# A two-layer encoder step on one core: part of the retention scores in float32r halves, 32 stationary columns for the sample, shared temporaries

## The chip, the cores and the metric

The kernel runs on one core of one Trainium2 chip. The metric is the device time in microseconds (us) of one execution. The time before is the median of three runs, 2776.84 us (2776.18 to 2777.35).

## What is computed

The reference is one inference step of a two-layer encoder on 256 prompt frames and 32 sample frames, 2048 wide. Layer 0 mixes frames by a gated MLP, layer 1 by retention; each is followed by a SwiGLU block, and every sublayer by a layer norm. The change lies in the retention of layer 1, which per head does, for one block of frames:

```python
q = rope(heads(q, RET_DK), pos) * (RET_DK ** -0.5)
k = rope(heads(k, RET_DK), pos)
...
scores = jnp.einsum('bhqd,bhkd->bhqk', q, k) * decay[None]
intra = jnp.einsum('bhqk,bhkv->bhqv', scores, v)
cross = jnp.einsum('bhqd,bhdv->bhqv', q, s0) * inner[None, :, :, None]
s_new = blk_decay[None, :, None, None] * s0 + jnp.einsum(
    'bhkd,bhkv->bhdv', k * zeta[None, :, :, None], v)
```

There are 8 heads with 256 channels of q and k and 512 of v. The kernel takes the prompt's 256 frames in one piece and the sample's 32 frames beside them, so 288 columns go through everything.

## The kernel before

**Matmuls in halves.** All large matmuls run on float32r operands, a float32 format that TensorE (PE) streams in one pass. To keep accuracy, an operand is split into a high half (`hi`, a cast on ScalarE, ACT) and a low half (`lo = x - hi`, a subtraction on VectorE, DVE); `split` at L449 to L451 does both. A product is then three matmuls: hi by hi, hi by lo, lo by hi (L106 to L108). The weights arrive in chunks of eight 128x128 blocks; `prep` loads a chunk three chunks ahead and splits it into `whi` and `wlo`. `turned` and `mm4` (L171 to L179) only give the moving columns another order of reading.

**Order of work.** PE's order is that of the code. A "tick" passes after each output tile of 128 rows (16 steps of three matmuls, L106 to L108); `core.after(n, f)` calls `f` n ticks later, so that the short matmuls of a head stand between the tiles of the large projection `ab_in`. The order on DVE and ACT is made by a scheduler when the kernel is built; the rows of the trace stand in that order.

**A head of the retention** (class `Head`). `evac` gets the finished tiles. When both tiles of k, and then of q, are done, `turn` rotates them (`rope`, L661 to L669, on DVE) into `r` (`rk`, `rq`); with k it starts `k_move`, which sends k through DRAM to have it by rows (`kw`). With q it makes the scaled sample's q (`qf`, and its halves `qi`), and asks for `scores` after two ticks (three for head 0). `k_split` (L741 to L759) makes the scaled halves `kh`, `kl`, `ks` from `kw`, also after two ticks. `scores` (L761) issues three groups of float32 matmuls into one PSUM bank: keys 0 to 127 with all 256 queries (L766), keys 128 to 255 with the second 128 queries (L768), and the sample's 32 frames (L770), for which `rk` held the sample's k three times side by side, so that 96 stationary columns give the scores on three groups of 32 partitions. The results are multiplied by the decay table (`pf`, `psf`) and split into `ph`, `pl` and `pss` (shown as `r_ps`), from which `attend`, one tick later, computes the outputs.

**Temporaries.** `prev` is the layer norm ahead of the retention; `prev.tmp` gives a buffer of 288 columns out of six that are used in turn. In the kernel before, the retention had buffers of its own for `zero`, `rt1`, `rt2`, `qf`, `pf` and `psf`.

Of the kernel before, what the change touches and what calls it, by code (L numbers as in the profile page):

```python
# [10 lines left out]
F32 = mybir.dt.float32  # L11
# [616 lines left out]
def retention(core, cst, x, y, lnp, prev, ins, st_p_out, st_s_out):  # L628
# [4 lines left out]
    with ExitStack() as es:  # L633
# [14 lines left out]
        zero = pool.tile([P, NS], F32, name="r_zero")  # L648
# [12 lines left out]
        def rope(dst, a, b, cos, sin, nm):  # L661
            t1 = pool.tile([P, NT], F32, tag="rt1", name=f"rt1{nm}", bufs=1)
            t2 = pool.tile([P, NT], F32, tag="rt2", name=f"rt2{nm}", bufs=1)
            nc.vector.tensor_tensor(t1, a[:, :NT], cos, ALU.mult)
            nc.vector.tensor_tensor(t2, b[:, :NT], sin, ALU.mult)
            nc.vector.tensor_tensor(dst[:, 0, :NT], t1, t2, ALU.subtract)
            nc.vector.tensor_tensor(t1, a[:, :NT], sin, ALU.mult)
            nc.vector.tensor_tensor(t2, b[:, :NT], cos, ALU.mult)
            nc.vector.tensor_tensor(dst[:, 1, :NT], t1, t2, ALU.add)  # L669

        class Head:
# [33 lines left out]
            def turn(self, m, ps):  # L705
                h = self.h
                isk = m >= 16
                nm = ("k" if isk else "q") + str(h)
                r = pool.tile([P, 2, NP + (NR if isk else NS)], F32, tag="kr" if isk else "qr", name="r" + nm)
                rope(r, ps[0], ps[1], cs[:, 0, :], cs[:, 1, :], nm)  # L710
                if isk:
                    self.kr = r
                    nc.scalar.copy(r[:, :, NT:].rearrange("p d (r n) -> p d r n", r=2),
                                   r[:, :, NP:NT].unsqueeze(2).broadcast_to([P, 2, 2, NS]))
                    self.k_move()
                else:
                    self.qr = r
                    qf = pool.tile([P, 2, NS], F32, tag="qf", name=f"qf{h}")
                    qi = pool.tile([P, 160], F32R, tag="qi", name=f"qi{h}")
                    self.qi = qi[:, 20:20 + 4 * NS].rearrange("p (d a n) -> p d a n", d=2, a=2)  # L720
                    nc.vector.tensor_tensor(qf, r[:, :, NP:], inn[:, h, :].unsqueeze(1).broadcast_to([P, 2, NS]), ALU.mult)
                    split(nc, self.qi[:, :, 0, :], self.qi[:, :, 1, :], qf)
                    core.after(self.wait, self.scores)
# [37 lines left out]
            def scores(self):  # L761
# [3 lines left out]
                for d in range(2):  # L765
                    mm(b[:, 0:NP], self.kr[:, d, 0:P], self.qr[:, d, 0:NP], start=d == 0, stop=d == 1)  # L766
                for d in range(2):
                    mm(b[:, NP:NP + P], self.kr[:, d, P:NP], self.qr[:, d, P:NP], start=d == 0, stop=d == 1)  # L768
                for d in range(2):
                    mm(b[:NR, 384:384 + NS], self.kr[:, d, NP:], self.qr[:, d, NP:], start=d == 0, stop=d == 1)  # L770
                pf = pool.tile([P, 384], F32, tag="pf", name=f"pf{h}")
                self.ph = pool.tile([P, 384], F32R, tag="ph", name=f"ph{h}")
                self.pl = pool.tile([P, 384], F32R, tag="pl", name=f"pl{h}")
                psf = pool.tile([P, NS], F32, tag="psf", name=f"psf{h}")
                nc.vector.tensor_tensor(pf[:, :NP], b[:, :NP], self.dec[:, :NP], ALU.mult)
                nc.vector.tensor_tensor(pf[:, NP:], b[:, NP:384], self.dec[:, :P], ALU.mult)
                nc.vector.tensor_tensor(psf[:NR, :], b[:NR, 384:384 + NS], self.dec[:NR, NP:], ALU.mult)
                r = slice(2 * NS, NR)
                nc.scalar.copy(pss[:NR, :NS], psf[:NR, :])
                nc.vector.tensor_tensor(pss[r, :NS], psf[r, :], pss[r, :NS].bitcast(F32), ALU.subtract)  # L780
                split(nc, self.ph, self.pl, pf)
# [278 lines left out]
```

## Time and profile before

| | |
|---|---|
| median of three runs | 2776.84 us |
| the profiled execution, its own time | 2779.29 us |
| its span, first to last instruction | 2777.5 us |
| granted TensorE clock, mean | 0.999 |
| PE, busy share of the span | 100% |
| DVE, busy share | 60% |
| ACT, busy share | 45% |
| scores, first to last start on PE | 1212.3 to 1810.3 us |

A row of the order of time has the start, the duration, the engine (PE for matmuls, PEld for their weight loads), the line, the operation, and what is written from what; `x4` are four equal instructions merged, and a bracket holds the idle time ahead and what ended it. A group's row has its busy time and the mean duration in ns behind the first bar. A row of stretches has the length and then, for PE, PEld, DVE, ACT and POOL, the busy time and the count, the granted clock, the DMA share and GB/s. Matmuls overlap, so the distance between starts says what a matmul costs PE, and the duration does not.

### The profile page before, as it was taken

Reading aid. Unit: us, or ns where it says so; the run is one execution under the profiler, and the core shown is the slowest. Engines: PE = TensorE matmul, PEld = TensorE weight load, DVE = VectorE, ACT = ScalarE, POOL = GpSimd, SP = SyncE. Lnnn points to the kernel's source line nnn. Section 1 sums busy time; section 2 is a strip of 40 time slices with the busy share of each in tenths; the row PEclk is TensorE's granted clock in tenths of the full one; section 3 lists DMA queues with packets and bytes.
Section 4 is the critical chain, followed back from the end, with each engine's and each line's share of the span. In section 5 each row is a group of like instructions: output and inputs, shape, how many; then the busy total and the mean of one; then the engine's idle time right before and its main releaser. Section 6 shows DMA issues by size and latency. Waiting matters only on the chain.

```text
span 2777.5 us, 51381 instructions
## 1 busy us (share of the span) xinstructions
PE 2764.5 (100%) x21574; PEld 2750.9 (99%) x21574; DVE 1665.4 (60%) x2358; ACT 1241.7 (45%) x1645; POOL 141.3 (5%) x241
## 2 busy tenths in 40 slices
PE   9999999999999999999999999999999999999998
PEld 9999999999999999999999999999999999999998
DVE  5688854445444466767765666767844445444465
ACT  5465643433334344644543444445633433333343
POOL 1100000000000000012200111200000000000001
PEclk9999999999999999999999999999999999999999
DMA  7655455555555555567765666755555555555553
GB/s 270 217 189 166 166 178 175 172 172 174 175 175 175 172 175 178 189 205 236 230 198 173 200 216 214 232 194 175 168 174 174 175 174 173 172 173 175 175 174 126
DMA packets 147672, 515.49 MB, mean 186 GB/s; under 512 B 18080, under 2 KB 22448, under 8 KB 147408
## 3 DMA queue, kind: packets, MB, share of 16 engines
q1 hardware_dynamic: 133072, 473.47, 51.1%
q0 software_dynamic: 14224, 38.59, 4.7%
q8 instruction: 168, 2.75, 0.4%
q14 instruction: 64, 0.52, 0.0%
q10 hardware_dynamic: 144, 0.15, 0.0%
HBM read 486.98 MB, written 25.17 MB: 184 GB/s over the span
## 4 chain that ended last, share of the span: by engine, by line
PE 98%; DVE 1%; DMA 1%; issue 0%; ACT 0%; POOL 0%; SPq 0%; DVEq 0%; POOLq 0%
PE af_in L107 13%; PE af_in L108 13%; PE af_in L106 13%; PE ab_in L106 7%; PE ab_in L107 7%; PE ab_in L108 7%; PE af_out L106 6%; PE af_out L107 6%; PE af_out L108 6%; PE ab_out L107 2%; PE ab_out L106 2%; PE ab_out L108 2%; PE aa_in L108 2%; PE aa_in L106 2%; PE aa_in L107 2%; PE aa_out L106 1%
## 5 line engine op out<-in xcount | busy, mean ns | idle before, releaser
L451 DVE TENSOR_TENSOR wlo<-raw,whi 128x1024 fp32r<-128x1024 f32 (+1 forms) x892 | 1086.0, 1218 | 883.6 <-ACT whi L450 879.4
L450 ACT CAST whi<-raw 128x1024 fp32r<-128x1024 f32 (+1 forms) x892 | 933.1, 1047 | 1382.8 <-issue 336.5
L107 PE MATMUL af_in<-xl,whi 128*128 128x288 f32 (+1 forms) x2816 | 812.6, 289 | 0.0
L106 PE MATMUL af_in<-xh,whi 128*128 128x288 f32 (+1 forms) x2816 | 812.3, 288 | 0.0
L108 PE MATMUL af_in<-xh,wlo 128*128 128x288 f32 (+1 forms) x2816 | 812.3, 288 | 0.0
L108 PEld LDWEIGHTS af_in<-xh,wlo 128*128 128x128 f32 x2816 | 527.7, 187 | 0.0
L107 PEld LDWEIGHTS af_in<-xl,whi 128*128 128x128 f32 x2816 | 527.7, 187 | 0.0
L106 PEld LDWEIGHTS af_in<-xh,whi 128*128 128x128 f32 x2816 | 527.7, 187 | 0.0
L106 PE MATMUL ab_in<-xh,whi 128*128 128x288 f32 (+1 forms) x1536 | 443.9, 289 | 0.0
L107 PE MATMUL ab_in<-xl,whi 128*128 128x288 f32 (+1 forms) x1536 | 443.3, 289 | 0.0
L108 PE MATMUL ab_in<-xh,wlo 128*128 128x288 f32 (+1 forms) x1536 | 443.2, 289 | 0.0
L108 PE MATMUL af_out<-hh,wlo 128*128 128x288 f32 x1408 | 405.9, 288 | 0.0
L106 PE MATMUL af_out<-hh,whi 128*128 128x288 f32 x1408 | 405.9, 288 | 0.0
L107 PE MATMUL af_out<-hl,whi 128*128 128x288 f32 x1408 | 405.9, 288 | 0.0
L107 PEld LDWEIGHTS ab_in<-xl,whi 128*128 128x128 f32 x1536 | 287.9, 187 | 0.3
L106 PEld LDWEIGHTS ab_in<-xh,whi 128*128 128x128 f32 x1536 | 287.9, 187 | 0.3
L108 PEld LDWEIGHTS ab_in<-xh,wlo 128*128 128x128 f32 x1536 | 287.9, 187 | 0.0
L107 PEld LDWEIGHTS af_out<-hl,whi 128*128 128x128 f32 x1408 | 263.8, 187 | 0.0
L108 PEld LDWEIGHTS af_out<-hh,wlo 128*128 128x128 f32 x1408 | 263.8, 187 | 0.0
L106 PEld LDWEIGHTS af_out<-hh,whi 128*128 128x128 f32 x1408 | 263.8, 187 | 0.0
L108 PE MATMUL aa_in<-xh,wlo 128*128 128x288 f32 x512 | 148.4, 290 | 1.2 <-DVE wlo L451 1.2
L106 PE MATMUL aa_in<-xh,whi 128*128 128x288 f32 x512 | 148.7, 290 | 0.1
(240 smaller groups left out, 2867.0 us busy)
## 6 DMA issues: line engine op xcount, KB each, us to landing
raw<-in_wpack_dram SPq DMA_DIRECT2D x887, 512.0 KB, 3.3
v_room<-tv POOLq DMA_DIRECT2D x32, 144.0 KB, 5.0
of<-o_room POOLq DMA_DIRECT2D x32, 144.0 KB, 5.3
vw<-v_room POOLq DMA_DIRECT2D x8, 512.0 KB, 5.3
out_st_s_dram<-sso POOLq DMA_DIRECT2D x16, 256.0 KB, 2.6
out_st_p_dram<-so POOLq DMA_DIRECT2D x16, 256.0 KB, 2.9
o_room<-to POOLq DMA_DIRECT2D x8, 512.0 KB, 3.8
y<-in_xT_dram SPq DMA_DIRECT2D x8, 288.0 KB, 5.5
```

The costliest lines, as they stand in the source:

```text
L106: mm(ps, hi, xh, start=first, stop=False)
L107: mm(ps, hi, xl, start=False, stop=False)
L108: mm(ps, lo, xh, start=False, stop=last)
L450: nc.scalar.copy(hi, f)
L451: nc.vector.tensor_tensor(lo, f, hi.bitcast(F32), ALU.subtract)
```

## The change

Three things change. The scores of the first 128 keys, two float32 matmuls (four passes in the trace, since each float32 matmul shows as two) become six float32r matmuls: k's columns 0 to 127 and q's columns 0 to 255 are split into halves (`k1a`, `k1b`, `q1a`, `q1b` for head 1; `a` is the high half). The sample's scores take 32 stationary columns and not 96, so k's threefold copy goes, and the three partition groups of `pss` are filled from one result of 32 partitions. The small temporaries come from `prev.tmp`; `pf` becomes two tiles, split one after the other.

PE's order at head 1, before and then after (`sc` is the bank of the scores):

```order
L108 MATMUL ab_in_192_14178<-xh,wlo_14106 128x3x24x4
L766 MATMUL sc_14244<-rq_14164,rk_14002 128x256 x2
L768 MATMUL sc_14244<-rq_14164,rk_14002 128x128 x2
L770 MATMUL sc_14244<-rq_14164,rk_14002 96x32 x2
L106 MATMUL ab_in_193_14262<-xh,whi_14135 128x3x24x4
```

```order
L108 MATMUL ab_in_192_14200<-xh,wlo_14124 128x3x24x4
L179 MATMUL sc_14266<-q1a,k1a 128x4x16x4
L179 MATMUL sc_14266<-q1b,k1a 128x4x16x4
L179 MATMUL sc_14266<-q1a,k1b 128x4x16x4
L179 MATMUL sc_14266<-q1a,k1a 128x4x16x4
L179 MATMUL sc_14266<-q1b,k1a 128x4x16x4
L179 MATMUL sc_14266<-q1a,k1b 128x4x16x4
L773 MATMUL sc_14266<-rq_14182,rk_14017 128x128 x2
L775 MATMUL sc_14266<-rq_14182,rk_14017 32x32 x2
L106 MATMUL ab_in_193_14292<-xh,whi_14153 128x3x24x4
```

The place among the tiles of the projection is the same; the first operands are now halves, and `q1b` is read by the second matmul.

DVE's order at head 1, from the last step of q's rotation to the first product with the decay, before and then after (`tv` is a transposition of the next projection tile, `wlo` a weight chunk's low half):

```order
L669 TENSOR_TENSOR rq_14164<-rt1q_14165,rt2q_14166 128x288
L721 TENSOR_TENSOR qf_14173<-rq_14164,r_inn 128x64
L451 TENSOR_TENSOR wlo_14211<-raw_14209,whi_14210 128x1024
L752 SCALAR_TENSOR_TENSOR kl_14091<-kw_14015,r_zt,kh_14090 128x128 x4
L758 SCALAR_TENSOR_TENSOR ks_14092<-kw_14015,r_zt,ks_14092 32x128 x2
L451 TENSOR_TENSOR qi_14174<-qf_14173,qi_14174 128x2x32
L696 STREAM_TRANSPOSE tv_14242<-ab_in_192_14178 128x9x32
L451 TENSOR_TENSOR wlo_14265<-raw_14263,whi_14264 128x1024
L775 TENSOR_TENSOR pf_14251<-sc_14244,dec_13280 128x256
```

```order
L669 TENSOR_TENSOR rq_14182<-rt1q_1_14185,rt2q_1_14186 128x288
L722 TENSOR_TENSOR qf_1_14193<-rq_14182,r_inn 128x64
L451 TENSOR_TENSOR wlo_14233<-raw_14231,whi_14232 128x1024
L755 SCALAR_TENSOR_TENSOR kl_14109<-kw_14031,r_zt,kh_14108 128x128 x4
L761 SCALAR_TENSOR_TENSOR ks_14110<-kw_14031,r_zt,ks_14110 32x128 x2
L451 TENSOR_TENSOR qi_14194<-qf_1_14193,qi_14194 128x2x32
L451 TENSOR_TENSOR q1b<-rq_14182,q1a 128x512
L696 STREAM_TRANSPOSE tv_14264<-ab_in_192_14200 128x9x32
L451 TENSOR_TENSOR wlo_14295<-raw_14293,whi_14294 128x1024
L780 TENSOR_TENSOR pf_1_14277<-sc_14266,dec_13283 128x256
```

One row is new, `q1b`, behind `kl`, `ks` and `qi`. In all of heads 1 to 7 `q1b`'s counterpart stands right behind `qi`, which is right behind `ks`.

ACT's order at head 1 and, behind the dots, at head 2, both after the change:

```order
L450 CAST whi_14232<-raw_14231 128x1024
L450 CAST qi_14194<-qf_1_14193 128x2x32
L450 CAST q1a<-rq_14182 128x512
L753 ACTIVATE kh_14108<-kw_14031,r_zt 128x256 x2
L759 ACTIVATE ks_14110<-kw_14031,r_zt 32x256 x2
L450 CAST whi_14294<-raw_14293 128x1024
...
L450 CAST whi_14931<-raw_14930 128x1024
L753 ACTIVATE kh_14807<-kw_14730,r_zt 128x256 x2
L759 ACTIVATE ks_14809<-kw_14730,r_zt 32x256 x2
L450 CAST qi_14893<-qf_1_14892 128x2x32
L450 CAST q2a<-rq_14881 128x512
L450 CAST whi_14993<-raw_14992 128x1024
```

`q1a` and `q2a` are the new rows; the others stand in the same order as before, so that in heads 1, 4, 5 and 6 `kh` and `ks` come behind the new cast, and in heads 2, 3 and 7 ahead of it.

```diff
@@ -645,7 +645,7 @@
         nc.gpsimd.dma_start(inn, ins["inner"])
         ln = PostNorm(core, cst, x, y, lnp, 2)
         pss = pool.tile([P, 2 * NS], F32R, tag="pss", name="r_ps")
-        zero = pool.tile([P, NS], F32, name="r_zero")
+        zero = prev.tmp("r_zero")[:, :NS]
         nc.gpsimd.memset(zero, 0.0)
         nc.scalar.copy(pss[:NR, NS:], zero[:NR, :])
         heads = {}
@@ -659,8 +659,8 @@
             return t[:, :4 * NT].rearrange("p (b i s) -> p b i s", b=9, i=4)
 
         def rope(dst, a, b, cos, sin, nm):
-            t1 = pool.tile([P, NT], F32, tag="rt1", name=f"rt1{nm}", bufs=1)
-            t2 = pool.tile([P, NT], F32, tag="rt2", name=f"rt2{nm}", bufs=1)
+            t1 = prev.tmp(f"rt1{nm}")
+            t2 = prev.tmp(f"rt2{nm}")
             nc.vector.tensor_tensor(t1, a[:, :NT], cos, ALU.mult)
             nc.vector.tensor_tensor(t2, b[:, :NT], sin, ALU.mult)
             nc.vector.tensor_tensor(dst[:, 0, :NT], t1, t2, ALU.subtract)
@@ -706,20 +706,23 @@
                 h = self.h
                 isk = m >= 16
                 nm = ("k" if isk else "q") + str(h)
-                r = pool.tile([P, 2, NP + (NR if isk else NS)], F32, tag="kr" if isk else "qr", name="r" + nm)
+                r = pool.tile([P, 2, NT], F32, tag="kr" if isk else "qr", name="r" + nm)
+                parts = [pool.tile([P, 2, P if isk else NP], F32R, tag=nm[0] + x, name=nm + x) for x in "ab"]
                 rope(r, ps[0], ps[1], cs[:, 0, :], cs[:, 1, :], nm)
                 if isk:
                     self.kr = r
-                    nc.scalar.copy(r[:, :, NT:].rearrange("p d (r n) -> p d r n", r=2),
-                                   r[:, :, NP:NT].unsqueeze(2).broadcast_to([P, 2, 2, NS]))
                     self.k_move()
+                    self.kp = parts
+                    split(nc, *parts, r[:, :, :P])
                 else:
                     self.qr = r
-                    qf = pool.tile([P, 2, NS], F32, tag="qf", name=f"qf{h}")
+                    qf = prev.tmp(f"qf{h}")[:, :2 * NS].rearrange("p (d n) -> p d n", d=2)
                     qi = pool.tile([P, 160], F32R, tag="qi", name=f"qi{h}")
                     self.qi = qi[:, 20:20 + 4 * NS].rearrange("p (d a n) -> p d a n", d=2, a=2)
                     nc.vector.tensor_tensor(qf, r[:, :, NP:], inn[:, h, :].unsqueeze(1).broadcast_to([P, 2, NS]), ALU.mult)
                     split(nc, self.qi[:, :, 0, :], self.qi[:, :, 1, :], qf)
+                    self.qp = parts
+                    split(nc, *parts, r[:, :, :NP])
                     core.after(self.wait, self.scores)
 
             def proceed(self, what, i=3):
@@ -762,23 +765,26 @@
                 h = self.h
                 self.proceed("s")
                 b = core.bank(f"sc{h}")
-                for d in range(2):
-                    mm(b[:, 0:NP], self.kr[:, d, 0:P], self.qr[:, d, 0:NP], start=d == 0, stop=d == 1)
+                (kh, kl), (qh, ql) = self.kp, self.qp
+                prods = [(l[:, d, :], r[:, d, :]) for d in range(2) for l, r in ((kh, qh), (kh, ql), (kl, qh))]
+                for i, (l, r) in enumerate(prods):
+                    mm4(b[:, 0:NP], l, r, start=i == 0, stop=i == len(prods) - 1)
                 for d in range(2):
                     mm(b[:, NP:NP + P], self.kr[:, d, P:NP], self.qr[:, d, P:NP], start=d == 0, stop=d == 1)
                 for d in range(2):
-                    mm(b[:NR, 384:384 + NS], self.kr[:, d, NP:], self.qr[:, d, NP:], start=d == 0, stop=d == 1)
-                pf = pool.tile([P, 384], F32, tag="pf", name=f"pf{h}")
+                    mm(b[:NS, 384:384 + NS], self.kr[:, d, NP:], self.qr[:, d, NP:], start=d == 0, stop=d == 1)
+                pf = [prev.tmp(f"pf{h}{i}") for i in range(2)]
                 self.ph = pool.tile([P, 384], F32R, tag="ph", name=f"ph{h}")
                 self.pl = pool.tile([P, 384], F32R, tag="pl", name=f"pl{h}")
-                psf = pool.tile([P, NS], F32, tag="psf", name=f"psf{h}")
-                nc.vector.tensor_tensor(pf[:, :NP], b[:, :NP], self.dec[:, :NP], ALU.mult)
-                nc.vector.tensor_tensor(pf[:, NP:], b[:, NP:384], self.dec[:, :P], ALU.mult)
-                nc.vector.tensor_tensor(psf[:NR, :], b[:NR, 384:384 + NS], self.dec[:NR, NP:], ALU.mult)
-                r = slice(2 * NS, NR)
-                nc.scalar.copy(pss[:NR, :NS], psf[:NR, :])
-                nc.vector.tensor_tensor(pss[r, :NS], psf[r, :], pss[r, :NS].bitcast(F32), ALU.subtract)
-                split(nc, self.ph, self.pl, pf)
+                psf = prev.tmp(f"psf{h}")[:, :NS]
+                nc.vector.tensor_tensor(pf[0][:, :NP], b[:, :NP], self.dec[:, :NP], ALU.mult)
+                nc.vector.tensor_tensor(pf[1][:, :P], b[:, NP:384], self.dec[:, :P], ALU.mult)
+                nc.vector.tensor_tensor(psf[:NS, :], b[:NS, 384:384 + NS], self.dec[:NS, NP:], ALU.mult)
+                for r in range(2):
+                    nc.scalar.copy(pss[r * NS:(r + 1) * NS, :NS], psf[:NS, :])
+                nc.vector.tensor_tensor(pss[2 * NS:NR, :NS], psf[:NS, :], pss[:NS, :NS].bitcast(F32), ALU.subtract)
+                split(nc, self.ph[:, :NP], self.pl[:, :NP], pf[0][:, :NP])
+                split(nc, self.ph[:, NP:], self.pl[:, NP:], pf[1][:, :P])
 
             def v_move(self):
                 h = self.h
```

## The prediction

> **What bounds the kernel now.** I read the page first, for the engine that sets the end; then TensorE's order of time around one head's scores; then VectorE and ScalarE in the same microseconds, because the new matmuls read what these two make.
>
> ```profile
> span 2777.5 us, 51381 instructions
> PE 2764.5 (100%) x21574; PEld 2750.9 (99%) x21574; DVE 1665.4 (60%) x2358; ACT 1241.7 (45%) x1645; POOL 141.3 (5%) x241
> PE 98%; DVE 1%; DMA 1%; issue 0%; ACT 0%; POOL 0%; SPq 0%; DVEq 0%; POOLq 0%
> ```
>
> TensorE (PE) is busy all the time and is 98% of the chain that ends last. So a nanosecond taken from PE's stream is a nanosecond of the kernel, and so is every nanosecond that PE is made to wait. VectorE (DVE, 60%) and ScalarE (ACT, 45%) have room on average; what counts is whether they have it at the moment when PE asks. The profiled execution took 2779.29 us, 1.79 more than its span; the three timed runs have a median of 2776.84, 2.45 below it. I add the sum to the median.
>
> **The matmuls (a gain).** In head 1 the scores stand on PE like this (start, duration, both in us; x4 are four passes merged in one row), and one stretch without any such work gives the pace of the 288-column matmuls:
>
> ```profile
> 1274.79 0.29 PE L108 MATMUL ab_in<-xh,wlo 128*128 128x288 f32 x1
> 1274.92 1.02 PE L766 MATMUL sc<-rq,rk 128*128 128x256 f32 x4
> 1275.79 0.61 PE L768 MATMUL sc<-rq,rk 128*128 128x128 f32 x4
> 1276.23 0.45 PE L770 MATMUL sc<-rq,rk 128*96 128x32 f32 x4
> 1276.51 0.38 PE L106 MATMUL ab_in<-xh,whi 128*128 128x288 f32 x1
> 1276.73 0.29 PE L107 MATMUL ab_in<-xl,whi 128*128 128x288 f32 x1
> ```
>
> ```profile
> 20.00:100.00 80.00, 80.00 (x634) 80.00 (x633) 48.86 (x70) 38.38 (x54) 11.32 (x18) 1.00 0.80 272
> ```
>
> The four float32 passes over 256 columns take 1275.79 - 1274.92 = 0.87 us, 0.22 each. They become six float32r matmuls of one pass. No float32r matmul of 256 columns in this arrangement is in the trace; the nearest are 288 columns, 80 us / 634 = 0.126 us from start to start, and 512 columns. The groups below give the durations; a weight load's row has its columns behind the star.
>
> ```profile
> L179 PE MATMUL sp<-vv,kh 128*128 128x512 f32 x64 | 19.2, 380 | 0.0
> L179 PEld LDWEIGHTS os<-whi,qi x16: 134/136/138, 1220.1 to 1817.0; 128*64 128x64 f32 x16
> L770 PEld LDWEIGHTS sc<-rq,rk 128*96 128x96 f32 x32 | 3.6, 164 | 0.0
> L451 DVE TENSOR_TENSOR vv<-vz,vv 32x512 fp32r<-32x512 f32 x8 | 5.4, 681 | 0.2
> L451 DVE TENSOR_TENSOR pl<-pf,ph 128x384 fp32r<-128x384 f32 x8 | 4.5, 559 | 3.9 <-ACT ph L450 3.9
> L450 ACT CAST vv<-vz 32x512 fp32r<-32x512 f32 x8 | 4.9, 614 | 0.3 <-DMA vz<-v_room 0.3
> ```
>
> 512 columns last 380 ns and 288 last 290, so a column is 0.40 ns and 256 columns come to 0.126 - 32 x 0.0004 = 0.113 us. Six are 0.68: a gain of **0.19 us** a head. Bounds: 0.126 each (0.11 gained) and half a float32 pass, 0.109 (0.22 gained).
>
> The sample's four passes stream only 32 columns, 0.28 us from 1276.23 to 1276.51. Most of that is weight loading: 64 columns load in 136 ns and 96 in 164, 0.87 ns a column, so 32 columns would load 0.056 us faster. The first load lies under the passes ahead of it; three are exposed: **0.16 us** a head. Bounds: nothing, and 0.17. Together 0.35 x 8 heads = **2.8 us gained**, between 0.9 and 3.1.
>
> One rule of the Trainium skill would cut this term ("TensorE: Matmul & The Clock Gate", section "Wait — 56ns, not 53.3ns?"): with hardware decode off a matmul costs about 62 ns to issue, however small. No row here shows that floor, since 0.28 us over four passes is 70 ns each and explained by the loads; by it the exposed passes would gain some 0.07 us a head, the term would be about 2.1, and the time 0.7 us higher, inside the range.
>
> **The new wait (a loss, and the larger term).** PE used to need only the rotated q (rq), which DVE finishes early. Now the second of the six matmuls needs q's low half (`q1b`), made by DVE from q's high half (`q1a`), made by ACT. The order printed above puts `q1b` on DVE behind kl x4, ks x2 and qi. Head 1, DVE and then ACT:
>
> ```profile
> 1272.53 0.23 DVE L721 TENSOR_TENSOR qf<-rq,r_inn 128x64 f32<-128x64 f32 x1
> 1273.04 1.23 DVE L451 TENSOR_TENSOR wlo<-raw,whi 128x1024 fp32r<-128x1024 f32 x1 [0.29 <-ACT whi L450]
> 1274.18 1.13 DVE L752 SCALAR_TENSOR_TENSOR kl<-kw,r_zt,kh 128x128 fp32r<-128x128 f32 x4
> 1275.33 0.60 DVE L758 SCALAR_TENSOR_TENSOR ks<-kw,r_zt,ks 32x128 fp32r<-32x128 f32 x2
> 1275.97 0.22 DVE L451 TENSOR_TENSOR qi<-qf,qi 128x64 fp32r<-128x64 f32 x1
> 1276.11 0.47 DVE L696 STREAM_TRANSPOSE tv<-ab_in 128x288 f32<-128x288 f32 x1
> ```
>
> ```profile
> 1271.95 1.06 ACT L450 CAST whi<-raw 128x1024 fp32r<-128x1024 f32 x1 [1.94 <-PE ab_in L107]
> 1272.91 0.24 ACT L450 CAST qi<-qf 128x64 fp32r<-128x64 f32 x1
> 1273.09 0.91 ACT L750 ACTIVATE kh<-kw,r_zt 128x256 fp32r<-128x256 f32 x2
> 1273.90 1.03 ACT L756 ACTIVATE ks<-kw,r_zt 32x256 fp32r<-32x256 f32 x2
> ```
>
> The instruction ahead of `q1b`, qi, starts at 1275.97 in the kernel before: 1.05 us *after* PE began the scores. That already decides the sign. Step by step: `q1a` takes kh's place on ACT at 1273.09 and lasts 0.61 (128x512; the nearest cast has 512 elements a partition too). kh follows at 1273.60 (rows overlap by 0.1), so everything on ACT shifts by 0.51 and its ks ends at 1274.93 + 0.51 = 1275.44. DVE's ks waits for that; a released DVE row starts 0.03 after (1273.01 to 1273.04), so at 1275.47 and not 1275.33: 0.14 later. qi starts at 1276.11, `q1b` 0.14 behind it (as tv does now) at 1276.25, and with 0.68 us it ends at **1276.93**. PE wanted it for its second matmul, at 1274.92 + 0.11 = 1275.03.
>
> What PE loses when DVE releases it late is shown by one of the few stalls of the trace:
>
> ```profile
> 135.40 1.22 DVE L451 TENSOR_TENSOR wlo<-raw,whi 128x1024 fp32r<-128x1024 f32 x1
> 136.68 0.19 PEld L108 LDWEIGHTS aa_in<-xh,wlo 128*128 128x128 f32 x1 [0.77 <-DVE wlo L451]
> 135.85 0.29 PE L107 MATMUL aa_in<-xl,whi 128*128 128x288 f32 x1
> 136.92 0.29 PE L106 MATMUL aa_in<-xh,whi 128*128 128x288 f32 x1
> ```
>
> DVE ends at 136.62, the load starts 0.06 later, and the matmul after that one starts 0.24 behind the load instead of 0.13, since the load is no longer hidden. So 0.16 is added: head 1 waits 1276.93 + 0.16 - 1275.03 = **2.06 us**. The order gives heads 4, 5 and 6 the same queues as head 1.
>
> In heads 2, 3 and 7 ACT runs kh and ks first and `q2a` behind qi, so nothing on DVE shifts ahead of qi. Head 2 (DVE, PE, ACT), and head 7 as the last of them:
>
> ```profile
> 1332.52 0.23 DVE L451 TENSOR_TENSOR qi<-qf,qi 128x64 fp32r<-128x64 f32 x1
> 1331.48 0.38 PE L766 MATMUL sc<-rq,rk 128*128 128x256 f32 x1
> 1330.67 1.03 ACT L756 ACTIVATE ks<-kw,r_zt 32x256 fp32r<-32x256 f32 x2
> 1331.72 0.24 ACT L450 CAST qi<-qf 128x64 fp32r<-128x64 f32 x1
> ...
> 1809.85 0.22 DVE L451 TENSOR_TENSOR qi<-qf,qi 128x64 fp32r<-128x64 f32 x1
> 1808.80 0.38 PE L766 MATMUL sc<-rq,rk 128*128 128x256 f32 x1
> ```
>
> `q2a` ends near 1331.87 + 0.61 = 1332.48, `q2b` runs from 1332.66 to 1333.34; PE wanted it at 1331.59: 1333.34 + 0.16 - 1331.59 = **1.91 us**. Head 7 has the same 1.05 between scores and qi. Head 0 does not wait, since its qi is long made:
>
> ```profile
> 1193.35 0.22 DVE L451 TENSOR_TENSOR qi<-qf,qi 128x64 fp32r<-128x64 f32 x1
> 1212.29 1.03 PE L766 MATMUL sc<-rq,rk 128*128 128x256 f32 x4
> ```
>
> Sum: 4 x 2.06 + 3 x 1.91 = **14.0 us lost**. Nothing hides it, as PE has no slack to give back. `q1b` is not in the trace; its bounds are 0.56 (384 elements) and 1.23 (1024), and the exposed load may cost nothing, so the term lies between 12.4 and 17.8.
>
> **The rest, at nothing.** The k halves (128x256) are made when the k of the head is rotated, a tile or more before the scores, and replace a ScalarE copy of k. The work behind the scores grows by two small casts and a second subtraction, some 0.5 us; behind the scores stand 16 steps of three matmuls, 48 x 0.126 = 6 us, before PE reads it, and it ends about 4 us into them. The tv and wlo that queue behind `q1b` on DVE are for tiles whose PE work is itself 2 us later. The shared temporaries are reused after six allocations, by instructions that stand behind their readers. If this cover failed, each head would add what is missing to its wait.
>
> **Rivals.** (1) *The halves are in time* (not slower): if `q1b` ran right behind qf, cast at 1272.76 and subtracted at about 1273.4, it would be done by 1274.1 and PE would not wait. Price: only the matmul term, 2776.84 - 2.8 = 2774.0, within 0.2%. It decides at 1275.0; qi's own row, 1.05 us too late, speaks against it in every head but the first. 4%. (2) *The clock drops after each wait*. The trace knows a slower pace of the array and a stall without it:
>
> ```profile
> 1.01 5.06 PE L955 MATMUL warm<-one 128*128 128x128 f32 x22 [1.01 <-POOL g_nrm L499]
> 130.00:145.00 15.00, 14.11 (x108) 13.61 (x107) 14.73 (x36) 14.80 (x29) 0.00 (x0) 1.00 0.60 191
> ```
>
> At the very start 22 passes over 128 columns take 5.06 us, 0.23 each, against 0.11 for L768's; that half pace lasts some 5 us. If each of seven waits brought it back, it would cost 2.5 us each: 2788.0 + 17.5 = 2805. Against it: the stall at 135.85 was 0.83 us long, and the rows behind it keep 0.13 apart. The Trainium skill has the rule for this (the same page, "Part 1: The HAM clock gate (the "warmup" mystery)"): the slower clock comes back after an idle window of about 3.4 us. A wait of 2 us stays under it; the short stall agrees, but no run here shows one of 2 us. 6%. (3) *The added ACT and DVE work delays the weights' halves too*: some 1 us a head more, 2796. ACT stands idle 1.94 before its whi above, so 3%.
>
> **How the numbers follow.** Forecast, 87%: 2776.84 - 2.8 + 14.0 = **2788.0 us**, 0.4% slower. Its own ends are 2776.84 + 12.4 - 3.1 = 2786.1 and 2776.84 + 17.8 - 0.9 = 2793.7; the upper one needs a 1.23 us subtraction of half the size, so I ask 2785.0 to 2793.0 for 8 in 10. 0.2% is 5.6 us, about what a measurement of this kernel can tell from no change. Slower than that: forecast, rivals 2 and 3, less a small part where waits come out half as long: 0.93. Within: rival 1 and that part, 0.06. Faster by 5.6 us would need more than all the matmul gain: 0.01.
>
> **What would show it.** Among the waits, PE's second score matmul waits for DVE's low half of q seven times, 1.9 to 2.1 us each, and PE's idle time grows by 14 us; score passes of six at 0.113; the last four passes in 0.12 us. Wrong would be: no such wait, matmuls 0.2 apart behind it, or PE waiting for whi or wlo.

## The result, and the profile after

The changed kernel took 2804.82 us (median of 6 runs, 2795.50 to 2809.51) beside 2777.02 us of the kernel before (6 runs, 2776.18 to 2778.18): 1.0098 of it, 95% interval 1.0087 to 1.0108. That is 27.8 us slower, where 11.2 had been forecast; the range ended at 2793. The runs of the changed kernel are 14 us apart, those of the kernel before 2.

The page of the changed kernel (its profiled execution took 2804.51 us):

```profile
span 2802.7 us, 51462 instructions
PE 2779.7 (99%) x21590; PEld 2764.9 (99%) x21590; DVE 1675.3 (60%) x2382; ACT 1248.2 (45%) x1669; POOL 141.0 (5%) x241
```

PE's busy time grew by 15.2 us although the change adds only 16 matmul passes. So waits are not all of it.

**The waits are there.** PE's waits in the changed kernel (engine, line, what it waited for, us in total, times, longest):

```profile
PE sc L179 <- DVE q1b L451: 2.0, 1, 2.0
PE sc L179 <- DVE q5b L451: 1.7, 1, 1.7
PE sc L179 <- DVE q4b L451: 1.5, 1, 1.5
PE sc L179 <- DVE q6b L451: 1.5, 1, 1.5
PE sc L179 <- ACT q7a L450: 1.5, 1, 1.5
...
PE sc L179 <- ACT q3a L450: 1.0, 1, 1.0
PE sc L179 <- DVE q2b L451: 0.9, 1, 0.9
PE sc L179 <- ACT q2a L450: 0.5, 1, 0.5
PE sc L179 <- DVE q3b L451: 0.4, 1, 0.4
PE sc L179 <- DVE q7b L451: 0.3, 1, 0.3
```

Seven heads wait, head 0 does not, 11.3 us in all. In heads 2, 3 and 7 PE waits first for the high half, so already ahead of the first score matmul. Head 1's scores on PE, and the queue on DVE in the same microseconds:

```profile
1271.82 0.27 PE L179 MATMUL sc<-q1a,k1a 128*128 128x256 f32 x1
1274.09 0.38 PE L179 MATMUL sc<-q1b,k1a 128*128 128x256 f32 x1 [2.00 <-DVE q1b L451]
1274.31 0.28 PE L179 MATMUL sc<-q1a,k1b 128*128 128x256 f32 x1
...
1274.78 0.60 PE L773 MATMUL sc<-rq,rk 128*128 128x128 f32 x4
1275.32 0.31 PE L775 MATMUL sc<-rq,rk 128*32 128x32 f32 x4
1275.56 0.40 PE L106 MATMUL ab_in<-xh,whi 128*128 128x288 f32 x1
1275.80 0.29 PE L107 MATMUL ab_in<-xl,whi 128*128 128x288 f32 x1
```

```profile
1271.43 1.14 DVE L755 SCALAR_TENSOR_TENSOR kl<-kw,r_zt,kh 128x128 fp32r<-128x128 f32 x4 [0.23 <-ACT kh L753]
1272.59 0.61 DVE L761 SCALAR_TENSOR_TENSOR ks<-kw,r_zt,ks 32x128 fp32r<-32x128 f32 x2
1273.21 0.22 DVE L451 TENSOR_TENSOR qi<-qf,qi 128x64 fp32r<-128x64 f32 x1
1273.35 0.68 DVE L451 TENSOR_TENSOR q1b<-rq,q1a 128x512 fp32r<-128x512 f32 x1
```

`q1b` starts behind `kl`, `ks` and `qi`, 1.53 us after PE began, and lasts 0.68 us, as predicted. From the last tile matmul ahead of the scores to the second one behind them, less two spacings of 127 ns, a group took 1.683 us before; in the start times of the trace to the ns it now takes 1.572 in head 0 and 3.38 to 3.91 in heads 1 to 7. Over eight heads that is **+13.1 us**; the prediction's own two terms gave 11.2.

**A slower pace follows some heads.** The first two rows are the kernel before, in two stretches of pure 288-column tiles; the next two are the same stretches of the changed kernel (length, PE's busy time and count, granted clock, DMA share, GB/s):

```profile
1230.00:1265.00 35.00, 35.00 (x278) 1.00 0.76 236
1410.00:1580.00 170.00, 170.00 (x1345) 1.00 0.58 187
```

```profile
1230.00:1265.00 35.00, 35.00 (x279) 1.00 0.80 241
1410.00:1580.00 170.00, 170.00 (x1277) 1.00 0.55 175
```

In 170 us the changed kernel makes 68 matmuls fewer, at a granted clock of 1.00 in both and with no wait. In the start times they stand 133.3 ns apart instead of 126.7. This slow stretch goes from head 3's attend group to head 4's scores (1405 to 1605 us), a second one from head 5's to head 6's (1700 to 1775); the 1230 stretch, behind head 0, is as before. Together, with the two attend groups at their start, that is **+13.5 us**.

**A low clock follows one wait.** Behind head 3's wait the tiles stand 0.24 us apart, and the stretch that holds them has a granted clock of 0.50:

```profile
1392.27 0.44 PE L106 MATMUL ab_in<-xh,whi 128*128 128x288 f32 x1
1392.50 0.44 PE L107 MATMUL ab_in<-xl,whi 128*128 128x288 f32 x1
```

```profile
1392.49:1395.90 3.41, 3.41 (x16) 0.50 0.61 197
```

Fourteen matmuls at 240 ns cost **+1.6 us**. Last, the profiled execution before had stalls near the start that this one lacks, **-3.0 us** (first fence before, second after); so the profile before took 2.3 us more than the median of its kernel.

```profile
5.00:20.00 15.00, 14.59 (x103) 1.00 0.75 266
130.00:145.00 15.00, 14.11 (x108) 1.00 0.60 191
```

```profile
5.00:20.00 15.00, 15.00 (x115) 1.00 0.90 312
130.00:145.00 15.00, 15.00 (x121) 1.00 0.61 186
```

13.1 + 13.5 + 1.6 - 3.0 = 25.2, which is the difference of the spans, 2802.7 - 2777.5. Half of the slowdown is the pace, of which the prediction has no word. The first theory was that the waits bring it (theory 1); the rivals were the new matmuls (rival 2) and the new places of the buffers (rival 3). These are the experiments' rivals and not those of the prediction, which has numbers of its own.

### The profile page after: what moved, and what is told of

Read it like the earlier page. It is cut to its first block, busy times and chain, and to the rows that moved or that the text cites. A ratio compares the mean times of both kernels' runs of the same rounds, so it can differ in the third digit from the quotient of the medians.

```text
span 2802.7 us, 51462 instructions
## 1 busy us (share of the span) xinstructions
PE 2779.7 (99%) x21590; PEld 2764.9 (99%) x21590; DVE 1675.3 (60%) x2382; ACT 1248.2 (45%) x1669; POOL 141.0 (5%) x241
## 4 chain that ended last, share of the span: by engine, by line
PE 98%; DVE 1%; DMA 0%; ACT 0%; issue 0%; POOL 0%; DVEq 0%; ACTq 0%; POOLq 0%
PE af_in L108 13%; PE af_in L106 13%; PE af_in L107 13%; PE ab_in L106 7%; PE ab_in L107 7%; PE ab_in L108 7%; PE af_out L107 6%; PE af_out L108 6%; PE af_out L106 6%; PE ab_out L107 2%; PE ab_out L108 2%; PE ab_out L106 2%; PE aa_in L108 2%; PE aa_in L107 2%; PE aa_in L106 2%; PE aa_out L108 1%
## 5 line engine op out<-in xcount | busy, mean ns | idle before, releaser
L108 PE MATMUL ab_out<-r_oh,wlo 128*128 128x288 f32 x512 | 149.6, 292 | 0.0
L107 PE MATMUL ab_out<-r_ol,whi 128*128 128x288 f32 x512 | 149.6, 292 | 0.0
```

The lines of the kernel that those rows point to most:

```text
L107: mm(ps, hi, xl, start=False, stop=False)
L108: mm(ps, lo, xh, start=False, stop=last)
```

## The experiments

Ratios are to the kernel before on the same chip, with their 95% intervals. "Slow behind" counts the attend groups, out of eight, behind which the profiled execution goes at 133.3 ns.

| kernel | median us | ratio | slow behind |
|---|---|---|---|
| halves_in_time | 2784.74 | 1.0030 (1.0019 to 1.0040) | 0 |
| wait_alone | 2806.47 | 1.0102 (1.0087 to 1.0116) | 2 |
| columns_alone | 2807.00 | 1.0107 (1.0092 to 1.0121) | 8 |
| buffers_alone | 2804.12 | 1.0096 (1.0083 to 1.0109) | 7 |
| moved_128 | 2804.40 | 1.0099 (1.0084 to 1.0115) | 7 |
| buffers_at_place | 2776.97 | 1.0002 (0.9993 to 1.0010) | 0 |
| columns_at_place | 2807.64 | 1.0112 (1.0098 to 1.0126) | 8 |
| scores_later | 2795.15 | 1.0067 (1.0054 to 1.0080) | 4 |
| moved_256 | 2776.08 | 0.9998 (0.9989 to 1.0007) | 0 |
| moved_q_only | 2776.07 | 0.9998 (0.9989 to 1.0006) | 0 |
| moved_k_128_q_256 | 2804.27 | 1.0095 (1.0082 to 1.0109) | 6 |
| key_state_last | 2777.25 | 1.0001 (0.9992 to 1.0010) | 0 |
| halves_later_96 | 2802.27 | 1.0092 (1.0078 to 1.0106) | 7 |
| changed_state_last | 2795.33 | 1.0067 (1.0053 to 1.0080) | 0 |
| before_state_last | 2776.86 | 1.0014 (0.9991 to 1.0037) | 0 |
| later_state_last | 2775.86 | 1.0000 (0.9991 to 1.0008) | 0 |
| later_96_state_last | 2776.90 | 1.0001 (0.9992 to 1.0010) | 0 |
| columns_state_last | 2777.80 | 1.0003 (0.9994 to 1.0012) | 0 |

### The parts one by one

**halves_in_time**: q's low half ahead of the weighting of k.

```diff
-                core.after(self.wait, self.k_split)
+                core.after(self.wait + 1, self.k_split)
```

> The changed kernel with the weighting of the keys' rows (k_split) asked for one step later, so that VectorE makes q's low half ahead of it; TensorE's instructions and their order stay those of the changed kernel. Theory 1 (the waits for q's low half cost the time, 14 us themselves and the rest by the slower pace and the low clock behind them): no wait over 0.2 us in the score groups, every 288-column stream 126.7 ns apart, 2776 us (2774.5 to 2777.5). Rival 2 (the mixture of float32r halves and of 32-column tiles brings the slower pace by itself): no waits, but stretches at 133.3 ns, 2780 to 2795 us. Rival 3 (the shared buffers do): the same as rival 2 here.

2784.74 us (2779.93 to 2795.71, ten runs). No slow stretch, but waits are left, which no theory had expected:

```profile
PE sc L179 <- ACT q1a L450: 2.2, 1, 2.2
...
PE sc L179 <- DVE q5b L451: 0.9, 1, 0.9
PE sc L179 <- DVE q1b L451: 0.7, 1, 0.7
...
PE sc L179 <- DVE q4b L451: 0.5, 1, 0.5
...
PE sc L179 <- DVE q6b L451: 0.2, 1, 0.2
```

So the place behind `kl` and `ks` was most of the lateness and not all of it: in heads 1, 4, 5 and 6 the halves are late even ahead of them. Behind head 1's two waits, 2.9 us in all, the granted clock was 0.50 for 6.8 us. It also speaks against rivals 2 and 3 as they were put, since the new matmuls and the new places are all in it.

**wait_alone**: float32 scores and 96 columns, as before, behind an operand that is made late (with the shared temporaries).

```diff
+                    self.q2 = q2 = pool.tile([P, 2, NP], F32, tag="q2", name=f"q2{h}")
+                    qc = pool.tile([P, 2, NP], F32, tag="qc", name=f"qc{h}")
+                    nc.scalar.copy(qc, r[:, :, :NP])
+                    nc.vector.tensor_tensor(q2, qc, r[:, :, :NP], ALU.max)
...
-                    mm(b[:, 0:NP], self.kr[:, d, 0:P], self.qr[:, d, 0:NP], start=d == 0, stop=d == 1)
+                    mm(b[:, 0:NP], self.kr[:, d, 0:P], self.q2[:, d, 0:NP], start=d == 0, stop=d == 1)
```

> The kernel before with the shared temporaries and with the 256-column score matmuls, still float32, reading a copy of q that ScalarE and then VectorE make at the place where the change makes q's halves; 96 stationary columns. Theory 1: seven waits of 1.5 to 2.2 us ahead of the score groups (14 us), behind some of them stretches at 133.3 ns, 2791 to 2811 us, with runs some us apart. Rival 2 (the new matmuls bring the slower pace): the waits alone, 126.7 ns everywhere, 2790 to 2792 us, runs within 1 us. Rival 3 (shared buffers): slow stretches here as well as with the shared buffers alone.

2806.47 us, five runs from 2799.02 to 2811.20; the profiled execution is the shortest of them. Its waits (the copy of q goes by the name q here), and one stretch behind head 5 (278 matmuls in 35 us at 126.7 ns, 264 here):

```profile
PE sc L770 <- DVE q L726: 12.0, 7, 1.8
```

```profile
1710.00:1745.00 35.00, 35.00 (x264) 1.00 0.69 207
```

Waits and shared temporaries give the changed kernel's time and its spread, with slow stretches behind heads 4 and 5. Up to here theory 1 held. The name says too much, though: the sharing moves a tile that PE reads by 128 bytes, and the next runs show that such a move brings slow stretches without any wait.

**columns_alone**: only the 32 stationary columns.

```diff
-                r = pool.tile([P, 2, NP + (NR if isk else NS)], F32, tag="kr" if isk else "qr", name="r" + nm)
+                r = pool.tile([P, 2, NT], F32, tag="kr" if isk else "qr", name="r" + nm)
...
-                    mm(b[:NR, 384:384 + NS], self.kr[:, d, NP:], self.qr[:, d, NP:], start=d == 0, stop=d == 1)
+                    mm(b[:NS, 384:384 + NS], self.kr[:, d, NP:], self.qr[:, d, NP:], start=d == 0, stop=d == 1)
```

> The kernel before with the sample's scores alone changed to 32 stationary columns. By the prediction's term (0.16 us less a head): 2775.7 us. By the changed kernel's trace (205 ns instead of 111 ahead of the first 32-column pass, 237 instead of 217 behind the last): 0.07 us more a head, 2777.6 us. Rival 2: stretches at 133.3 ns, 2780 us or more.

2807.00 us, four runs within 1.2 us, slow behind all eight heads, and no wait in the scores.

**buffers_alone**: only the shared temporaries.

```diff
-        zero = pool.tile([P, NS], F32, name="r_zero")
+        zero = prev.tmp("r_zero")[:, :NS]
...
-                pf = pool.tile([P, 384], F32, tag="pf", name=f"pf{h}")
+                pf = [prev.tmp(f"pf{h}{i}") for i in range(2)]
```

> The kernel before with the shared temporaries alone (the scores' product in two buffers, so split twice); matmuls as before. Theory 1 and rival 2: 2777.0 us, as before, 126.7 ns everywhere. Rival 3 (the buffers' places bring the slower pace): stretches at 133.3 ns, 2780 to 2795 us.

2804.12 us, four runs within 1.1 us, slow behind heads 1 to 7. Theory 1 falls with these two: parts without any wait, one of which changes nothing in PE's order, cost as much as the whole change, and the same in every run. Rival 3 was left, but it could not say why the columns did it too.

### The place of rk

A program fixes each tile's bytes. The shared temporaries free a row of 128 bytes ahead of the heads' buffers, so that `rk` (k rotated, which the scores load as weights) moves from byte 204864 of a partition to 204736. `rq` moves from 215360 to 212928. All that PE reads in the attend group stays where it was.

**moved_128**: the kernel before with this one edit; its instructions and their order are those of before.

```diff
-        zero = pool.tile([P, NS], F32, name="r_zero")
+        zero = pool.tile([P, 2 * NS], F32, name="r_zero")[:, :NS]
```

> The kernel before with one unused row of 128 bytes a partition ahead of the heads' buffers: the keys' and queries' tiles rk and rq, which the score matmuls read, lie 128 bytes further; every instruction and its order are the same, and everything that TensorE reads in the attend groups stays where it was. Theory A (the two buffers' places change by some ns how the score group leaves TensorE, and that picks the pace of 126.7 or 133.3 ns behind the next attend group): 2795 to 2807 us, with stretches at 133.3 ns from an attend group to the next scores. Rival B (another part of the shared temporaries, such as the product split in two or the order on VectorE and ScalarE, does): 2777 us, 126.7 ns throughout.

2804.40 us, four runs within 1.1 us. Its page and its pace:

```profile
PE 2790.4 (100%) x21574; PEld 2777.0 (99%) x21574; DVE 1665.7 (59%) x2358; ACT 1239.2 (44%) x1645; POOL 140.9 (5%) x241
```

```profile
1295.00:1325.00 30.00, 30.00 (x228) 1.00 0.79 247
1410.00:1580.00 170.00, 170.00 (x1277) 1.00 0.54 175
```

The count of PE's passes is that of before, 21574; the time went into the pace, in the stretches behind head 1 and head 3 here, and behind all heads from 1 on.

**buffers_at_place** is buffers_alone with two unused tiles that put `rk` and `rq` back to the bytes of before.

```diff
         zero = prev.tmp("r_zero")[:, :NS]
+        pool.tile([P, NS], F32, name="pad0")
...
+                if isk:
+                    pool.tile([P, 2 * NT], F32, tag="pad1", name=f"pad1{h}")
```

> The shared temporaries alone, as in buffers_alone, with two unused buffers that put rk and rq back to the bytes at which the kernel before has them. Theory A (the places of rk and rq): 2777 us, no stretch at 133.3 ns. Rival B (the sharing itself): 2804 us, slow behind every attend group but the first.

2776.97 us: sharing costs nothing.

**moved_256**, **moved_q_only** and **moved_k_128_q_256** move the two tiles by other amounts:

```diff
-        zero = pool.tile([P, NS], F32, name="r_zero")
+        zero = pool.tile([P, 3 * NS], F32, name="r_zero")[:, :NS]
```

> As moved_128, with two such unused rows: rk and rq lie 256 bytes further than in the kernel before. If only the place within 256 bytes counts: 2777 us, 126.7 ns throughout. If any move picks the pace anew: about 2804 us, or some other number of slow stretches, the same in every run.

```diff
+                if isk:
+                    pool.tile([P, NS], F32, tag="pad", name=f"pad{h}")
                 rope(r, ps[0], ps[1], cs[:, 0, :], cs[:, 1, :], nm)
```

> The kernel before with 128 unused bytes between rk and rq: rk, which is loaded as weights, stays at its bytes, and rq, which streams through, lies 128 bytes further. If rq's place picks the pace: 2804 us. If rk's does: 2777 us.

The third has the edits of moved_128 and of moved_q_only together.

> The kernel before with rk moved by 128 bytes and rq by 256, by unused rows; every instruction is the same. If rk's place within 256 bytes picks the pace: 2804 us, slow behind the attend groups from head 1 on, as moved_128. If rk and rq have to move by the same 128 bytes: 2777 us.

2776.08, 2776.07 and 2804.27 us. `rk` by 256 bytes is as before, `rq` alone by 128 as well, `rk` by 128 is slow at each of the places of `rq` that were tried. With `rq` at 256, though, head 1 was not slow in the profiled execution, which had not been expected. So it is the place of the tile loaded as weights, and 128 of 256 bytes make the difference; smaller steps were not tried. (The decay table and two more tiles lie ahead of `rk` and moved with it; PE reads none of them.)

**columns_at_place** keeps `rk` and `rq` of columns_alone at the bytes of before (`r` as wide as before, the 32 columns taken out of it as `self.kr[:, d, NP:NT]`).

> The sample's scores with 32 stationary columns, as in columns_alone, with rk and rq at the bytes at which the kernel before has them. If the places alone pick the pace: 2777.6 us (0.07 us more a head), 126.7 ns throughout. If the narrow tile picks it as well, by leaving TensorE at another point: 2807 us, slow behind all eight attend groups.

2807.64 us: the narrow tile brings the slow stretches by itself. A place and a tile's shape thus do the same thing without a wait. That a wait does it alone is not shown: in every kernel here that waits, `rk` lies 128 bytes off as well. What waits seem to change is which heads are slow: buffers_alone, with `rk` and `rq` at the same bytes as wait_alone, is slow behind seven heads and its runs are 1.1 us apart; wait_alone is slow behind two, and its runs are 12 us apart. What place, shape and wait can all change is when the stream reaches the attend group, 48 matmuls behind the scores.

### Where the pace is picked

In the start times of every trace, the stream reaches the attend group in one of two ways: the last tile matmul and the first of the group (`os`) take 127 to 128 and 236 to 237 ns, or 131 to 132 and 231 to 232. The sums are alike, so it is the start of the first `os` that lies some 4 to 5 ns later. In the 14 kernels that have the attend group in its first order, before and after among them, the first kind was followed by 126.7 ns in 61 of 61 heads and the second by 133.3 in 51 of 51. The first matmuls to run slower are the two of the sample's key state (`ss`, the sixth and seventh). Head 2's attend group before, and in moved_128:

```profile
1340.15 0.38 PE L179 MATMUL os<-wlo,qi 128*64 128x512 f32 x1
1340.37 0.61 PE L179 MATMUL ss<-vv,ks 96*128 96x512 f32 x2
1340.82 0.61 PE L179 MATMUL ob<-vv,ph 128*128 128x512 f32 x2
```

```profile
1340.33 0.38 PE L179 MATMUL os<-wlo,qi 128*64 128x512 f32 x1
1340.56 0.64 PE L179 MATMUL ss<-vv,ks 96*128 96x512 f32 x2
1341.03 0.61 PE L179 MATMUL ob<-vv,ph 128*128 128x512 f32 x2
```

From `ss` to `ob` it takes 0.45 us before and 0.47 in moved_128; single ones 219 and 236 ns apart. `ss` has 96 rows, and 128 rows precede and follow it. The first `os` has 96 rows too, so it is not shown that the number of rows is the reason.

**key_state_last**: moved_128 with `ss` at the end of the group.

```diff
-                for d in range(2):
-                    mm4(b[d], self.ks[:NR, d], self.vs[:NR, :], start=True, stop=True)
                 ob = self.outputs()
                 sp = self.states()
+                for d in range(2):
+                    mm4(b[d], self.ks[:NR, d], self.vs[:NR, :], start=True, stop=True)
```

> moved_128 with the two matmuls of the sample's key state (ss, 96 rows) moved from the sixth and seventh place of the attend group to its end. In the slow traces ss is the first that runs slower (236 instead of 219 ns). If ss at its place is where the pace is picked: 126.7 ns behind it and about 2777 us. If the pace comes with the stream from the scores, whatever stands in the attend group: 2804 us.

2777.25 us, and the stretches have the counts of the kernel before again:

```profile
1295.00:1325.00 30.00, 30.00 (x239) 1.00 0.85 267
1410.00:1580.00 170.00, 170.00 (x1344) 1.00 0.58 188
```

In this trace, though, all eight heads reach the group in the first way, so it could have been a change of the arrival again. It also says that the place of `rk` alone does not settle how a head arrives, since `rk` lies here as in moved_128.

**changed_state_last** is the changed kernel with the same edit; its waits differ from run to run, so its heads arrive in both ways.

> The changed kernel with the two ss matmuls at the end of the attend group, nothing else. Theory A (ss between os and ob lets the slow pace begin): no stretch at 133.3 ns in any run, the waits stay, so 2777 + 13.1 = 2790 us, a few us more where a wait is followed by matmuls at 240 ns. Rival B (the place only changed TensorE's point in moved_128): slow stretches behind some attend groups, other ones in every run, 2795 to 2810 us.

2795.33 us (2791.52 to 2800.56). Two heads of its profiled execution, 1 and 4, arrive in the second way (132 and 231, 132 and 232 ns), and behind both the stream goes at 126.7 ns.

**columns_state_last**, columns_at_place with the edit, settles it:

> columns_at_place with ss at the end of the attend group. If the slow pace of the narrow tile begins at ss as well: 126.7 ns throughout, and the tile's own price of 0.07 us a head is left, 2777.6 us. If the narrow tile slows the stream in another way: 2780 to 2808 us.

2777.80 us. All eight heads arrive in the second way, and none is slow behind. So `ss` at its old place is where the second way of arriving turns into 133.3 ns; behind the last of the group it doesn't; why the place in the group matters stays open. The control **before_state_last**:

> The kernel before with the two ss matmuls at the end of the attend group. Theory A: 2777 us, as before. Rival B: slow stretches may begin, up to 2807 us.

2776.86 us; ten of its runs lie between 2776.36 and 2778.46 and one at 2814.08, of which there is no trace. So "never slow" is shown for the profiled heads only (48 of 48 with `ss` last).

The time of changed_state_last was 5 us over its expectation of 2790 and within what the rival had asked, so the trace decides and not the time. Its profiled execution, the longest of the five (2800.56 us), shows the pace kept, longer waits, and the low clock behind three of them (heads 1, 4 and 6; the last in the second fence).

```profile
PE sc L179 <- DVE q6b L451: 2.7, 1, 2.7
PE sc L179 <- DVE q4b L451: 2.7, 1, 2.7
PE sc L179 <- DVE q1b L451: 2.5, 1, 2.5
```

```profile
1767.24:1770.65 3.41, 3.06 (x15) 0.50 0.27 91
1770.65:1774.06 3.41, 3.41 (x16) 0.50 0.44 153
```

Its score groups take 20.1 us more than those of before, and 240 ns spacings behind them another 3.3. In heads 1 and 4 the trace shows why the waits are longer. On ACT the cast of a weight chunk (`whi`) stands ahead of q's halves. There it had to wait for the chunk's DMA, and started 2.27 and 1.77 us ahead of the scores, where it was 2.92 and 3.09 in the changed kernel. Head 4's:

```profile
1594.11 1.05 ACT L450 CAST whi<-raw 128x1024 fp32r<-128x1024 f32 x1 [3.22 <-DMA raw<-in_wpack_dram]
```

Why that DMA came later was not tried.

### Without waits

**scores_later**: the scores of heads 1 to 7 one step later.

```diff
-                    core.after(self.wait, self.scores)
+                    core.after(3, self.scores)
```

> The changed kernel with the scores of heads 1 to 7 asked for one step later (as head 0's are), so that q's halves are there. If only the waits cost and the pace stays at 126.7 ns: 2776 us. If the pace is picked anew behind each score group: without waits the pick is the same in every run, so either 2776 us or, with slow stretches behind most attend groups, about 2800 us, within 1 us from run to run.

2795.15 us, five runs within 2.6 us; the expectation had 2776 or about 2800. PE waits nowhere in the scores, and a group takes 1.566 to 1.574 us beyond two spacings; but heads 1, 3, 5 and 7 arrive in the second way and are slow behind. In the stretch 1410 to 1580 us it has 1277 matmuls, as the changed kernel.

So the changed kernel goes slow without any wait as well, and its time then hardly differs from run to run.

**halves_later_96** has 96 columns again, from a threefold copy of k in a shared buffer:

```diff
+                    self.k3 = prev.tmp(f"k3{h}")[:, :2 * NR].rearrange("p (d n) -> p d n", d=2)
+                    nc.scalar.copy(self.k3.rearrange("p d (r n) -> p d r n", r=3),
+                                   r[:, :, NP:].unsqueeze(2).broadcast_to([P, 2, 3, NS]))
...
-                    mm(b[:NS, 384:384 + NS], self.kr[:, d, NP:], self.qr[:, d, NP:], start=d == 0, stop=d == 1)
+                    mm(b[:NR, 384:384 + NS], self.k3[:, d, :], self.qr[:, d, NP:], start=d == 0, stop=d == 1)
```

> The changed kernel with the scores of heads 1 to 7 one step later and with 96 stationary columns for the sample's scores, as before the change (a copy of k's last 32 columns, three times, in a shared buffer). No waits in the score groups; a score group takes 1.50 us beyond two spacings (1.683 before, less 0.18), so 2775.3 us if the pace stays at 126.7 ns behind every attend group, up to 2803 us if it is slow behind most; which of the two, the theory doesn't tell ahead.

2802.27 us, slow behind seven heads. With `ss` last both lose the slow stretches:

> The changed kernel with the scores of heads 1 to 7 one step later and ss last: no waits. Theory A: 126.7 ns throughout, a score group of 1.570 instead of 1.683 us beyond two spacings, 2776.1 us. Rival B: slow behind some attend groups, 2780 to 2800 us.

> halves_later_96 with ss last. Theory A: 126.7 ns throughout, a score group of 1.500 instead of 1.683 us beyond two spacings, 1.5 us less than before: 2775.5 us, the shortest. Rival B: slow behind some attend groups, 2780 to 2803 us.

2775.86 and 2776.90 us. The first is the best form of the change that was found; its expected gain of 0.9 us (eight groups of 1.573 instead of 1.683 us) is there in the trace, but the ratio, 1.0000 (0.9991 to 1.0008), can't tell it from the kernel before. In the second, head 7's group has 0.27 us of stall in the trace. No version beat the kernel before by more than can be measured.

## Why the prediction was wrong

- **The new wait (right).** 14.0 us lost were predicted in heads 1 to 7. The trace has waits in these seven heads and none in head 0. Groups 1 to 7 grew by 1.70 to 2.23 us (1.91 and 2.06 predicted); since the matmuls gained 0.11 in each of eight groups, the waits cost 13.1 + 0.9 = 14.0, of which 11.3 are in the list. The list counts from the modelled end of the matmul ahead, and in the start times the first spacing behind a wait is 217 to 224 ns instead of some 115, since the load there is no longer hidden. That the sums agree to 0.1 us is luck: in heads 2, 3 and 7 part of the wait is for the high half, which the prediction had in time, and in changed_state_last the same waits cost 21.
- **The six float32r passes (right).** 0.19 us a head; behind the wait they stand 115 to 120 ns apart in head 1, and halves_later_96, which has them without waits and with the old 96 columns, shows 0.18 (1.683 to 1.50).
- **The 32 columns (wrong size, wrong sign).** 0.16 us a head was to be gained in three exposed loads. The last two of the four passes did come closer (32 instead of 85 ns apart). But the first narrow pass starts 205 ns behind the pass ahead of it instead of 111, the second 52 to 53 behind the first instead of 29, the next tile matmul 126 behind the last narrow pass instead of 85, and the one after it 235 to 238 behind that instead of 217. The sum is a loss of 0.07 us a head (columns_state_last: 1.752 against 1.683). The rows show why: the narrow load starts with its own pass.

```profile
1274.67 0.53 PEld L773 LDWEIGHTS sc<-rq,rk 128*128 128x128 f32 x4
1275.32 0.20 PEld L775 LDWEIGHTS sc<-rq,rk 128*32 128x32 f32 x4
```

  In the kernel before, L770's first load started at 1276.12, 0.11 ahead of its pass at 1276.23; here both start at 1275.32. "The first load lies under the passes ahead of it" failed. With it the matmul term is 0.9 us and not 2.8.
- **"The rest, at nothing" and the sum (the step that failed).** The prediction charged the moved buffers only with being reused in time. It had no term for the stretches behind the scores, because it took the pace that it had read from one stretch, "0.126 us from start to start", for all of them. The pace turned out to have two values, and in the changed kernel's profiled run the slow one cost 13.5 us. columns_state_last shows where it is picked (`ss` at its old place), and changed_state_last that the changed kernel has no slow stretch with `ss` last. The place of `rk` (moved_128) and the narrow tile (columns_at_place) bring slow stretches without waits, and the changed kernel without waits still has them (scores_later). Which heads are slow differs with the waits; how much of the changed kernel's pick is due to them and how much to `rk` and the narrow tile was not separated.
- **The prediction's rival 2 (partly).** The low clock came back behind one wait of seven in the changed kernel, for 1.6 us where 2.5 was priced (there the matmuls stood 0.24 us apart, the prediction's own sign of it); behind three of seven in changed_state_last. The Trainium skill ("TensorE: Matmul & The Clock Gate", "Part 1: The HAM clock gate (the "warmup" mystery)") gives about 3.4 us both for the idle window that brings the slower clock back and for the time that it lasts. The second agrees with the changed kernel's trace (a granted clock of 0.50 for 3.41 us). The first does not: head 3's two waits, 1.0 and 0.4 us in the list, were enough, while head 1's 2.0 were not. By the clock records of the traces it matters where a wait falls. The half clock begins at 1392.49 us, 406 steps of 3.413 us behind the clock's first rise at 6.68, and the other traces with such a stretch have it on the same steps. In the start times head 3's idle time, 1.6 us, lies within one step, from 1389.08 to 1392.49; head 1's lies in two, 1.1 us in each.
- **The prediction's rivals 1 and 3.** Neither came: the halves were late, and PE waited for no `whi` or `wlo` in the heads.

## What to carry to other kernels

When one engine is busy all the time, its steady spacing is a term of its own: read it stage by stage before and after, by counts over a fixed stretch, since 5% over some 540 us (27 us in moved_128) outweighs seven waits (14 us). In this kernel a move of a tile by 128 bytes or a narrower weight tile flipped it, and no wait and no clock showed it; the remedy here was the order of the matmuls (the 96-row pair at the end of its group).

## What the runs showed of the hardware that was not expected

- A stream of 128x288 float32r matmuls has two steady spacings at a granted clock of 1.00: 126.7 and 133.3 ns. The slow one kept itself for up to 200 us, to the next scores. Which it takes depended here on a shift of some 4 to 5 ns in the arrival at a group, and on the place of two 96-row matmuls in that group.
- The place of a float32 weight tile in its partition can move that arrival: with the group in its first order 128 bytes changed it, 256 didn't; 128 bytes on the streamed operand did not.
- Going from 128 to 32 stationary columns costs 94 ns at the first narrow pass (205 instead of 111), as the narrow load starts with its own pass and not under the one ahead.
- A wait of 1.4 to 3 us sometimes brings half clock (240 ns a matmul): behind none of the seven waits in wait_alone, one in the changed kernel, one in halves_in_time, three in changed_state_last. It lasted 3.41 us in three of these five cases and twice that in two (head 6 of changed_state_last, head 1 of halves_in_time), and began on fixed steps of 3.413 us. In the step ahead of it PE was idle for 1.6 to 3.1 us; up to 1.96 us in a step of wait_alone did not bring it, so what is counted within a step is not known.
